# A hybrid encoder block on one core: one raw load queued earlier, another last tile, and another split of its normalisation

## The chip, the cores and the metric

The kernel runs on one core of one Trainium2 chip. A core has five engines with one in-order instruction stream each: TensorE (PE, matrix products; its weight loads are listed as PEld), VectorE (DVE), ScalarE (ACT), GpSimd (POOL) and SyncE (SP), which here issues nearly all DMAs. The metric is the device time of one execution in microseconds (us). Three runs of the kernel before gave 441.77, 443.6 and 445.18 us, a median of 443.6.

## The reference, cut to what matters

One layer on x of 1024 tokens by 1024 columns, in float32:

```
h = x @ W_in                        # sections q_a k_a v_a z_a q_b k_b v_b z_b
y_a = neighborhood_attention(...)   # 8 heads, 8 x 16 window on the 16 x 64 grid, relative bias
y_b = windowed_gqa_with_sink(...)   # 8 query heads, 2 key heads, |i - j| <= 128, rotary
mixed = concat([y_a * silu(z_a), y_b * silu(z_b)])
y = mixed @ W_out
x = layer_norm(2 ** 0.25 * x + y) * gain + bias
```

## The kernel before, in words

Every matrix operand is split into a high and a low float16 half (a "cast" or `hi` on ACT, a subtraction or `lo` on DVE or POOL), and a product of two operands is three PE instructions: high x high, high x low, low x high.

*Prologue.* Six projection groups run, counted in PE products (`run_to`). Small jobs hang on that count through `at(c, fn)`. `w_scale(NPRO)` (L805) is one: it multiplies the sums of the remaining weights' absolute values by a matrix of ones on PE and works out scales on DVE.

*Attention.* A loop over steps i = 0 to 137 (L1576) writes one attention unit of 128 queries per step into the engines' streams: scores on PE (L914, L915), row minimum on DVE (L928), exponential on ACT (L944), the split of the weights on ACT and DVE (L962, L963), a DMA transpose on SP (L965), the products with v (L991), the division (L1000, L1007), a transpose of the head group on PE (L1029) and its product with the gate z (L1035). There are 128 units; the steps after them finish what is in flight. PE's gaps between are filled with the projections and, from step 121 on, with the first products of the output projection.

Beside this, jobs stand in queues per engine. `pop` takes those of a small priority number; `fill_in` takes others when the planner's book says that the engine is free: it adds a cost to `due[engine]` for each job and compares it with `at_step(i)`, the time it gives step i. A job is ready once its dependencies were written out in an earlier step (two steps more behind a DMA) and are booked to be over; an SP entry waits until its dependency's booked end plus 1.0 lies behind. SP takes at most three entries a step from step 118 on, before that step's transpose.

*Output projection.* It is done in 2 x 2 blocks with seven products instead of eight (names q1 to q3, p4, q5 to q7 in `TERMS`, L1286), on sums S1 to S4 of the mixed blocks and T1 to T4 of the weight blocks, each over four parts i = 0 to 3 of the inner dimension. For i = 0 and 1 the T's come ready split (`t_soon`: tiles T of 512 KB). For i = 2 and 3 they come raw: `t_late_load(n)` (L1134) loads 256 KB into one of five buffers, and `t_late(n)` (L1143) queues the cast on ACT and the low half on POOL or DVE. Load n = 0 to 4 follow the weight splits; load 5 (T3, part 3) is queued in `late_loads` (L1560) in step 129 behind two T tiles and one x tile; 5, 6 and 7 each wait for the low half of load 0, 1 and 2, whose buffer they take.

*Closing.* `final` (L1317) is written out by hand. The output has eight row tiles; tile t (0 to 3) and tile 4 + t share their products. A product group is 12 PE instructions into one PSUM bank: `q5(t)`, `q6(t)`, `q7(t)`, `q3(t)`, `p4(t)`, `q2(t)`. `add` (L1333) adds a bank to the row tile in SBUF on DVE, `bn` takes statistics, `begin` aggregates them on DVE and takes the square root on ACT, `norm` normalises: for most tiles DVE does one half of the columns with gain and bias held in PSUM (`gp`, `bp`), and ACT and POOL do the other (`norm_half` multiplies by the gain, adds the bias and sends the half off on SP). For tiles 0, 3 and 4 ACT and POOL do both halves.

The last tile is tile 7. Its first half of columns gets its last product, p4(3), in three pieces of 256, 128 and 128 columns, with statistics by 128 columns. In `norm_last` (L1369) PE keeps itself going with 40 idle products (L1374), then normalises columns 512 to 1024 in PSUM as x * gain - mean * gain + sd * bias, by three pairs of products with diagonal matrices (L1375, L1384, L1385), and ACT scales them out in two pieces (L1391); DVE does columns 0 to 512 (L1386, L1388). `norm_ahead` (L1366) has multiplied the half by the gain on POOL, in between tile 3's instructions there. SP sends 512 and 256 columns, ACT's queue 256.

Of the kernel before, what the change touches and what calls it, by code (L numbers as in the profile page):

```python
# [13 lines left out]
ALU = mybir.AluOpType  # L14
# [56 lines left out]
def hybrid_block(ctx, tc, xT, x, wt, wv, wo, bias, sink, gain, lbias, cos, sin, bmask, out):  # L71
# [403 lines left out]
    with ExitStack() as vctx:  # L475
# [319 lines left out]
        def at(c, fn, *a):  # L795
            events.setdefault(c, []).append(lambda: fn(*a))
# [5 lines left out]
            at(30 + 8 * t, v_part, t)  # L802
        for i in range(NS):
            at(14 + 14 * i + {11: 6, 13: -2, 14: -16}.get(i, 0), sum_w, i)
        at(217, w_scale, NPRO)  # L805
        for c, o in zip((20, 28, 68, 76), T_SUM):
            at(c, t_add, *o)
        at(90, t_store)
# [508 lines left out]
    def final():  # L1317
# [23 lines left out]
        def bn(t, a, c):  # L1341
            o, w = c
            if t not in stats:
                stats[t] = fp.tile([128, 8, 6], F32, name=f"stats{t}", bufs=1)
            b = 128 if t == 7 else 512
            for i in range(w // b):
                n = (512 * a + o) // b + i
                nc.vector.bn_stats(stats[t][:, n, :], xrs[t][:, b * n:b * n + b])

        def row_stats(t):  # L1350
            mv = fp.tile([128, 2], F32, tag="mv", name="mv")
            nc.vector.bn_aggr(mv, stats[t][:, :8 if t == 7 else 2, :])  # L1352
# [8 lines left out]
            nc.vector.tensor_scalar(nmr, mv[:, 0:1], rstd, -1.0, op0=ALU.mult, op1=ALU.mult)  # L1361
            return rstd, nmr

        HP, H1 = slice(512, 1024), slice(0, 512)

        def norm_ahead(t):  # L1366
            nc.gpsimd.tensor_mul(xrs[t][:, HP], xrs[t][:, HP], gb[:, HP])
# [1 line left out]
        def norm_last(t):  # L1369
            ts = slice(128 * t, 128 * t + 128)  # L1370
            xr, pn = xrs[t], bank("t")
            busy = bank("s")
            for _ in range(40):
                nc.tensor.matmul(busy[:, :128], warm, warm, start=True, stop=True)  # L1374
            nc.tensor.matmul(pn, identf, xr[:, HP], start=True, stop=False)  # L1375
            dm, ds = (fp.tile([128, 128], F32, name=n, bufs=1) for n in ("dm", "ds"))
            mv = fp.tile([128, 2], F32, tag="mv", name="mv")
            nc.vector.bn_aggr(mv, stats[t])
            sd = fp.tile([128, 1], F32, tag="sd", name="sd")
            nc.scalar.activation(dm, nident, AF.Copy, scale=mv[:, 0:1])  # L1380
            nc.scalar.activation(sd, mv[:, 1:2], AF.Sqrt, bias=eps)
            nc.scalar.activation(ds, identf, AF.Copy, scale=sd)
            rstd = fp.tile([128, 1], F32, tag="rstd", name="rstd")
            nc.tensor.matmul(pn, dm, gb[:, HP], start=False, stop=False)  # L1384
            nc.tensor.matmul(pn, ds, bb[:, HP], start=False, stop=True)  # L1385
            nc.vector.scalar_tensor_tensor(xr[:, H1], xr[:, H1], mv[:, 0:1], gp, op0=ALU.subtract, op1=ALU.mult)  # L1386
            nc.vector.reciprocal(rstd, sd)
            nc.vector.scalar_tensor_tensor(xr[:, H1], xr[:, H1], rstd, bp, op0=ALU.mult, op1=ALU.add)  # L1388
            nc.sync.dma_start(out[ts, H1], xr[:, H1])
            for h, q in ((slice(512, 768), nc.sync), (slice(768, 1024), nc.scalar)):  # L1390
                nc.scalar.activation(xr[:, h], pn[:, h.start - 512:h.stop - 512], AF.Copy, scale=rstd)  # L1391
                q.dma_start(out[ts, h], xr[:, h])

        begun = []

# [6 lines left out]

        def norm(t, *st_):
            ts = slice(128 * t, 128 * t + 128)
            xr, ha, hb = xrs[t], slice(0, 512), slice(512, 1024)
            mv, sd = st_ or row_stats(t)
            rstd, nmr = row_scale(mv, sd)
            both = t in (0, 3, 4)
            h = slice(0, 1024) if both else hb
            nc.scalar.activation(xr[:, h], xr[:, h], AF.Identity, bias=nmr, scale=rstd)  # L1410
            if not both:
                nc.vector.scalar_tensor_tensor(xr[:, ha], xr[:, ha], mv[:, 0:1], gp, op0=ALU.subtract, op1=ALU.mult)
                nc.vector.scalar_tensor_tensor(xr[:, ha], xr[:, ha], rstd, bp, op0=ALU.mult, op1=ALU.add)
                nc.sync.dma_start(out[ts, ha], xr[:, ha])
            for h in (ha, hb) if both else (hb,):
                if t != 3:
                    norm_half(t, h)

        def norm_half(t, h, between=None):
            xr = xrs[t]  # L1420
            nc.gpsimd.tensor_mul(xr[:, h], xr[:, h], gb[:, h])  # L1421
            if between:
                between()
            nc.gpsimd.tensor_add(xr[:, h], xr[:, h], bb[:, h])
            nc.sync.dma_start(out[128 * t:128 * t + 128, h], xr[:, h])

# [34 lines left out]
        def q3(t):  # L1461
            run("q3", t, cb[t])
            add(t, 1, cb[t], whole=True)
            begin(t)
            if t > 1:
                finish()

        def p4(t):
            run("p4", t, b[t])
            add(4 + t, 0, b[t], whole=True)  # L1470
            begin(4 + t)
            if t > 1:
# [37 lines left out]
        q2(2)  # L1510
        q7(2)
        c11(2)
        q5(3)
        q3(2)
        q6(3)
        p4(2)
        q2(3)
        c11(3)
        q3(3)
        run("q7", 3, b[3])  # L1520
        add(7, 1, b[3])
        add(7, 0, b[3])
        bn(7, 1, (0, 512))
        norm_half(3, slice(0, 512), lambda: norm_ahead(7))
        norm_half(3, slice(512, 1024))
        for c, tag in ((0, 256), "t"), ((256, 128), "s"), ((384, 128), "t"):
            add(7, 0, run("p4", 3, bank(tag), None, c), c, whole=True)
        norm_last(7)

    def m_last(between):  # L1530
        z, za = zt[ZP[3][1]], zt[ZP[3][0]]
# [28 lines left out]
    def late_loads():  # L1560
        t_soon(0)
        x_soon(0)
        t_soon(3)
        t_late_load(5, t_fin[0])
        t_late(5)
        x_soon(4)
        x_soon(1)
        t_late_load(6, t_fin[1])
        t_soon(1)
        t_soon(2)  # L1570
        t_late_load(7, t_fin[2])

    sp_at = []
    clock["step"] = 0
# [1 line left out]
    for i in range(-LD, NU + LO):  # L1576
# [38 lines left out]
        if i == T_AT:  # L1615
            for n in range(5):
                t_late(n)
        if i == 129:
            late_loads()
        if bulk["last"] == i:  # L1620
# [127 lines left out]
```

## Time and profile before

| what | before |
|---|---|
| median of the three runs | 443.6 us |
| the profiled execution | 443.51 us |
| its span, first to last instruction | 441.7 us |
| mean granted clock of PE | 0.994 |
| busy: PE, DVE, ACT, POOL | 430.3, 350.3, 316.3, 295.1 us |
| start of the last output DMA | 437.97 us |

The profile lists, for one execution, when each instruction ran and what ended the idle time before it. In a row of the timeline stand the start, the length, the engine, the line, what it writes from what, and in brackets how long the engine had been idle and who released it. SPq and ACTq are the streams of SP and ACT where they issue DMAs. In the chain of waits stand the start, the length and the work in which the end was waited for.

### The profile page before, as it was taken

Reading aid. Unit: us, or ns where it says so; the run is one execution under the profiler, and the core shown is the slowest. Engines: PE = TensorE matmul, PEld = TensorE weight load, DVE = VectorE, ACT = ScalarE, POOL = GpSimd, SP = SyncE. Lnnn points to the kernel's source line nnn. Section 1 sums busy time; section 2 is a strip of 40 time slices with the busy share of each in tenths; the row PEclk is TensorE's granted clock in tenths of the full one; section 3 lists DMA queues with packets and bytes.
Section 4 is the critical chain, followed back from the end, with each engine's and each line's share of the span. In section 5 each row is a group of like instructions: output and inputs, shape, how many; then the busy total and the mean of one; then the engine's idle time right before and its main releaser. Section 6 shows DMA issues by size and latency. Waiting matters only on the chain.

```text
span 441.7 us, 9455 instructions
## 1 busy us (share of the span) xinstructions
PE 430.3 (97%) x3209; PEld 251.4 (57%) x3209; DVE 350.3 (79%) x870; ACT 316.3 (72%) x681; POOL 295.1 (67%) x303
## 2 busy tenths in 40 slices
PE   9999999999999999999999999999999997999995
PEld 8997754444455656565656565655555653444453
DVE  5988967775978778988898898879879864866684
ACT  4849789678688978888988778888888862743221
POOL 0110085797668656879989898777999796547245
PEclk9999999999999999999999999999999999899999
DMA  7951469995349999987889999898999699803122
GB/s 249 406 195 60 145 226 337 281 332 201 125 123 199 201 169 207 178 182 132 180 160 208 212 193 190 198 209 177 184 191 231 129 179 354 352 24 120 48 96 96
DMA packets 131409, 84.82 MB, mean 192 GB/s; under 512 B 97568, under 2 KB 106656, under 8 KB 131360
## 3 DMA queue, kind: packets, MB, share of 16 engines
q1 hardware_dynamic: 131216, 84.08, 77.0%
q8 instruction: 25, 0.41, 0.4%
q14 instruction: 24, 0.20, 0.1%
q10 hardware_dynamic: 144, 0.13, 0.1%
HBM read 50.60 MB, written 10.52 MB: 138 GB/s over the span
## 4 chain that ended last, share of the span: by engine, by line
PE 76%; DVE 7%; ACT 5%; issue 4%; POOL 4%; DMA 3%; DVEq 0%; POOLq 0%; SPq 0%; ACTq 0%
PE ps_pj L449 38%; PE ps_s L556 6%; PE ps_t L1300 5%; PE ps_t L991 5%; PE ps_pj L1300 5%; PE ps_s L1300 4%; PE ps_pj L556 3%; PE ps_t L556 3%; PE ps_s L915 3%; PE ps_s L914 3%; DVE split L963 2%; DMA tl<-tf 2%; DVE sn L928 1%; POOL tp L1097 1%; ACT ps_s L944 1%
## 5 line engine op out<-in xcount | busy, mean ns | idle before, releaser
L449 PE MATMUL ps_pj<-xf,wh 128*128 128x512 f16 x672 | 201.4, 379 | 0.0
L449 PE MATMUL ps_pj<-xf,wl 128*128 128x512 f16 x336 | 127.3, 379 | 0.0
L449 PEld LDWEIGHTS <-wh 128*128 128x128 f16 x672 | 63.8, 98 | 58.6 <-issue 0.5
L944 ACT ACTIVATE ps_s<-sn,nm 128x321 f32<-128x321 f32 (+3 forms) x128 | 67.7, 529 | 33.9 <-DVE nm L928 32.8
L963 DVE SCALAR_TENSOR_TENSOR split<-ps_s,split 128x320 f16<-128x320 f32 (+2 forms) x128 | 62.7, 490 | 22.1 <-ACT split L962 20.8
L252 POOL TENSOR_SCALAR wr<-wr,wsc 128x512 f32<-128x512 f32 x32 | 24.6, 768 | 57.7 <-ACT wh L247 53.8
L962 ACT ACTIVATE split<-ps_s 128x320 f16<-128x320 f32 (+2 forms) x128 | 55.0, 430 | 1.6
L449 PEld LDWEIGHTS <-wl 128*128 128x128 f16 x336 | 32.9, 98 | 37.8
L253 POOL TENSOR_TENSOR wl<-wr,wh 128x512 f16<-128x512 f32 x32 | 39.9, 1247 | 2.7
L914 PE MATMUL ps_s<-ks,qs 128*128 128x320 f16 (+3 forms) x128 | 38.2, 298 | 0.8 <-DVE split L963 0.8
L915 PE MATMUL ps_s<-ks,qs 128*128 128x320 f16 (+3 forms) x128 | 38.2, 298 | 0.0
L928 DVE CUSTOM_DVE_ANT_0 sn<-ps_s,bias,sg 128x368 f32<-128x368 f32 (+1 forms) x64 | 36.1, 563 | 2.6 <-PE ps_s L915 2.4
L991 PEld LDWEIGHTS <-tr 128*128 128x128 f16 (+1 forms) x1056 | 36.2, 98 | 2.4 <-issue 0.7
L928 DVE CUSTOM_DVE_ANT_0 sn<-ps_s,bm,nsk 128x320 f32<-128x320 f32 (+2 forms) x64 | 36.5, 571 | 0.5
L1300 PEld LDWEIGHTS <-m 128*128 128x128 f16 x192 | 18.1, 98 | 23.6 <-issue 3.9
L1421 POOL TENSOR_TENSOR xr<-xr,gb 128x512 f32<-128x512 f32 x10 | 12.7, 1274 | 24.1 <-ACT xr L1410 24.1
L366 POOL COPY ks<-ks 64x512 f16<-64x512 f16 x40 | 25.7, 643 | 3.9 <-ACT ks L310 1.8
L247 ACT ACTIVATE wh<-wr,wsc 128x512 f16<-128x512 f32 x32 | 22.7, 710 | 1.1 <-DVE wsc L277 1.1
L556 PEld LDWEIGHTS <-xf 128*128 128x128 f16 x192 | 18.6, 98 | 7.3
L915 PEld LDWEIGHTS <-qs 128*128 128x128 f16 x128 | 12.5, 98 | 16.2 <-issue 1.6
L1354 ACT ACTIVATE sd<-mv,eps 128x1 f32<-128x1 f32 x7 | 2.1, 295 | 27.1 <-DVE mv L1352 27.1
L914 PEld LDWEIGHTS <-qs 128*128 128x128 f16 x128 | 12.5, 98 | 15.1
(257 smaller groups left out, 966.3 us busy)
## 6 DMA issues: line engine op xcount, KB each, us to landing
wr<-in_wt SPq DMA_DIRECT2D x32, 256.0 KB, 3.1
ws<-in_wt SPq DMA_DIRECT2D x15, 512.0 KB, 5.6
wor<-in_wo SPq DMA_DIRECT2D x20, 256.0 KB, 3.9
xr<-in_x SPq DMA_DIRECT2D x8, 512.0 KB, 9.0
out<-xr SPq DMA_DIRECT2D x15, 256.0 KB, 2.0
bias<-in_bias SPq DMA_DIRECT2D x8, 440.0 KB, 4.2
wob<-in_wo SPq DMA_DIRECT2D x12, 256.0 KB, 3.9
wvraw<-in_wv SPq DMA_DIRECT2D x9, 320.0 KB, 5.6
```

Of the source, the lines that this page charges most:

```text
L253: nc.gpsimd.tensor_sub(l, raw, h)
L366: nc.gpsimd.tensor_copy(place(t, o, half, col), place(t, a, half, col))
L449: nc.tensor.matmul(ps, a[:, k % 4, :], mv, start=(k == 0 and i == 0), stop=(k == KT - 1 and i == 2))
L556: nc.tensor.matmul(ps[:, :320], lh[:, ts], rh[:, cs], start=(k == ko[0] and i == 0), stop=(k == ko[-1] and i == 2))
L914: nc.tensor.matmul(ps[:, :n], q, sl[0], start=True, stop=False)
L915: nc.tensor.matmul(ps[:, :n], q, sl[1], start=False, stop=True)
L928: nc.vector.tensor_tensor_reduce(sn[:, at0:at0 + n], ps[:, :n], bias_t, sg[:, c:c + 1], init, op0=ALU.add, op1=ALU.min, accum_out=nm)
L944: nc.scalar.activation(pt[:, c], sn[:, c], AF.Exp, bias=nm, scale=-1.0, accum_out=acc)
L962: nc.scalar.activation(h, pt[:, c], AF.Copy, scale=PSCALE)
L963: nc.vector.scalar_tensor_tensor(l, pt[:, c], PSCALE, h, op0=ALU.mult, op1=ALU.subtract)
L991: nc.tensor.matmul(ps[:, w * m:w * m + e], a, b_, start=(i == 0), stop=(i == len(mms) - 1))
L1300: nc.tensor.matmul(ps[:, cs], lh[:, 128 * t:128 * t + 128], rh[:, cs], start=(fresh and e == 0 and n == 0), stop=(e == len(terms) - 1 and ...
```

## The change

*Loads.* Load 5 and its split are queued in step 122, with the splits of loads 0 to 4, instead of in step 129. Loads 6 and 7 are queued one after the other behind one T tile more, ahead of the last T tile.

*Prologue.* `w_scale(NPRO)` hangs on count 224 instead of 217.

*Last tile.* Tile 3 is the last, not 7. Its q5 part is added on its own, q3(3) is the product done in three pieces at the end, and p4(3) and tile 7's statistics come earlier; tile 7 is now one of those that ACT and POOL normalise whole, and `norm_ahead` runs ahead of its four POOL instructions. In every other tile DVE's and ACT's halves change places.

*Split.* In `norm_last` PE normalises columns 0 to 384, and DVE the other 640: 512 as before, and 128 with gain and bias in a PSUM bank `gq`, filled by two ACT copies and also the target of the idle products. ACT scales PE's 384 columns out in one instruction and sends them on its own queue; SP sends 512 and 128.

```
-        at(217, w_scale, NPRO)
+        at(224, w_scale, NPRO)
...
-        HP, H1 = slice(512, 1024), slice(0, 512)
+        HP, HQ, H1 = slice(0, 384), slice(384, 512), slice(512, 1024)
...
-            busy = bank("s")
             for _ in range(40):
-                nc.tensor.matmul(busy[:, :128], warm, warm, start=True, stop=True)
-            nc.tensor.matmul(pn, identf, xr[:, HP], start=True, stop=False)
+                nc.tensor.matmul(gq[:, :128], warm, warm, start=True, stop=True)
+            nc.tensor.matmul(pn[:, HP], identf, xr[:, HP], start=True, stop=False)
...
-            nc.tensor.matmul(pn, dm, gb[:, HP], start=False, stop=False)
-            nc.tensor.matmul(pn, ds, bb[:, HP], start=False, stop=True)
-            nc.vector.scalar_tensor_tensor(xr[:, H1], xr[:, H1], mv[:, 0:1], gp, op0=ALU.subtract, op1=ALU.mult)
-            nc.vector.reciprocal(rstd, sd)
-            nc.vector.scalar_tensor_tensor(xr[:, H1], xr[:, H1], rstd, bp, op0=ALU.mult, op1=ALU.add)
-            nc.sync.dma_start(out[ts, H1], xr[:, H1])
-            for h, q in ((slice(512, 768), nc.sync), (slice(768, 1024), nc.scalar)):
-                nc.scalar.activation(xr[:, h], pn[:, h.start - 512:h.stop - 512], AF.Copy, scale=rstd)
-                q.dma_start(out[ts, h], xr[:, h])
+            nc.tensor.matmul(pn[:, HP], dm, gb[:, HP], start=False, stop=False)
+            nc.tensor.matmul(pn[:, HP], ds, bb[:, HP], start=False, stop=True)
+            halves = (H1, gp, bp), (HQ, gq[:, 128:256], gq[:, 256:384])
+            for h, g, _ in halves:
+                nc.vector.scalar_tensor_tensor(xr[:, h], xr[:, h], mv[:, 0:1], g, op0=ALU.subtract, op1=ALU.mult)
+                if h is H1:
+                    nc.vector.reciprocal(rstd, sd)
+            for h, _, o in halves:
+                nc.vector.scalar_tensor_tensor(xr[:, h], xr[:, h], rstd, o, op0=ALU.mult, op1=ALU.add)
+                if h is H1:
+                    nc.sync.dma_start(out[ts, h], xr[:, h])
+            nc.scalar.activation(xr[:, HP], pn[:, HP], AF.Copy, scale=rstd)
+            nc.sync.dma_start(out[ts, HQ], xr[:, HQ])
+            nc.scalar.dma_start(out[ts, HP], xr[:, HP])
...
-            xr, ha, hb = xrs[t], slice(0, 512), slice(512, 1024)
+            xr, ha, hb = xrs[t], slice(512, 1024), slice(0, 512)
...
-            both = t in (0, 3, 4)
+            both = t in (0, 4, 7)
...
+        gq = bank("s")
+        nc.scalar.copy(gq[:, 128:256], gb[:, HQ])
+        nc.scalar.copy(gq[:, 256:384], bb[:, HQ])
         q5(3)
+        add(3, 1, cb[3])
+        q6(3)
         q3(2)
-        q6(3)
+        q7(3)
         p4(2)
+        p4(3)
         q2(3)
         c11(3)
-        q3(3)
-        run("q7", 3, b[3])
-        add(7, 1, b[3])
-        add(7, 0, b[3])
-        bn(7, 1, (0, 512))
-        norm_half(3, slice(0, 512), lambda: norm_ahead(7))
-        norm_half(3, slice(512, 1024))
+        norm_ahead(3)
+        norm_half(7, slice(0, 512))
+        norm_half(7, slice(512, 1024))
         for c, tag in ((0, 256), "t"), ((256, 128), "s"), ((384, 128), "t"):
-            add(7, 0, run("p4", 3, bank(tag), None, c), c, whole=True)
-        norm_last(7)
+            add(3, 1, run("q3", 3, bank(tag), None, c), c, whole=True)
+        norm_last(3)
...
         t_soon(3)
-        t_late_load(5, t_fin[0])
-        t_late(5)
         x_soon(4)
         x_soon(1)
-        t_late_load(6, t_fin[1])
         t_soon(1)
+        for n in (6, 7):
+            t_late_load(n, t_fin[n - 5])
         t_soon(2)
-        t_late_load(7, t_fin[2])
...
             for n in range(5):
                 t_late(n)
+            t_late_load(5, t_fin[0])
+            t_late(5)
```

More of the change, by code (lines that the diff above doesn't have):

```diff
@@ L1344, in bn @@
                 stats[t] = fp.tile([128, 8, 6], F32, name=f"stats{t}", bufs=1)
-            b = 128 if t == 7 else 512
+            b = 128 if t == 3 else 512
             for i in range(w // b):
@@ L1351, in row_stats @@
             mv = fp.tile([128, 2], F32, tag="mv", name="mv")
-            nc.vector.bn_aggr(mv, stats[t][:, :8 if t == 7 else 2, :])
+            nc.vector.bn_aggr(mv, stats[t][:, :8 if t == 3 else 2, :])
             sd = fp.tile([128, 1], F32, tag="sd", name="sd")
@@ L1415, in norm, with norm_half @@
             for h in (ha, hb) if both else (hb,):
-                if t != 3:
+                if t != 7:
                     norm_half(t, h)
-        def norm_half(t, h, between=None):
+        def norm_half(t, h):
             xr = xrs[t]
             nc.gpsimd.tensor_mul(xr[:, h], xr[:, h], gb[:, h])
-            if between:
-                between()
             nc.gpsimd.tensor_add(xr[:, h], xr[:, h], bb[:, h])
```

## The prediction

> **What bounds the kernel now.** I read the page first, for the slices in which an engine is not full.
>
> ```profile
> PE   9999999999999999999999999999999997999995
> ACT  4849789678688978888988778888888862743221
> PEclk9999999999999999999999999999999999899999
> ```
>
> TensorE (PE) is full in all slices but two: the one from 364 to 375 us (a slice is 441.7 / 40 = 11.04 us) and the last. The granted clock dips in one slice, just behind the first of these, where ScalarE (ACT) falls to 2. So two places can give time: that hole and the tail. The second view is the chain of waits, at the hole.
>
> ```profile
> 363.32 7.59 DMA tl<-tf
> ...
> 373.69 2.75 PE ps_t L1300 x9
> ```
>
> The chain runs through one transfer, raw T load 5, for 7.59 us. Third, the timeline of the same place.
>
> ```profile
> 360.40 1.21 SPq L965 DMA_TRANSPOSE tr<-split  x1
> 361.65 0.58 SPq L1127 DMA_DIRECT2D T<-td  x1
> 361.74 0.62 ACT L1219 CAST s<-z 128x512 f16<-128x512 f32 x1 [1.90 <-DVE z L1242]
> 363.32 0.41 SPq L1139 DMA_DIRECT2D tl<-tf  x1
> 365.46 0.18 DVE L1000 RECIPROCAL ri<-ps_t 128x4 f32<-128x4 f32 x1 [0.28 <-PE ps_t L991]
> 365.68 0.42 DVE L1007 TENSOR_TENSOR on<-ps_t,ri 128x256 f32<-128x256 f32 x1
> 367.85 0.60 PE L1029 MATMUL ps_t<-identf,on 128*128 128x128 f32 x4
> 369.58 0.81 PE L1300 MATMUL ps_t<-tp,s 128*128 128x512 f16 x3
> 370.93 0.72 ACT L1149 ACTIVATE tp<-tl,wsn 128x512 f16<-128x512 f32 x1 [7.56 <-DMA tl<-tf]
> 371.56 0.60 ACT L1219 CAST z<-z 128x512 f16<-128x512 f32 x1
> 372.19 0.79 DVE L1222 TENSOR_TENSOR z<-z 128x512 f16<-128x512 f32 x1 [6.09 <-ACT z L1219]
> 372.90 0.74 DVE L1035 SCALAR_TENSOR_TENSOR z<-ps_t,zc,z 128x512 f32<-128x512 f32 x1
> 373.69 0.59 PE L1300 MATMUL ps_t<-T,m 128*128 128x512 f16 x2 [3.30 <-DVE z L1035]
> ```
>
> Fourth, the busy time by engine of the two stretches behind it (PE, PEld, DVE, ACT, POOL with their counts, then the granted clock, the DMA share and GB/s).
>
> ```profile
> 370.00:375.00 5.00, 1.70 (x9) 0.70 (x8) 2.81 (x5) 2.81 (x4) 3.17 (x3) 1.00 1.03 407
> 375.00:380.00 5.00, 5.00 (x17) 1.94 (x16) 4.96 (x6) 3.96 (x6) 2.72 (x3) 0.66 1.04 421
> ```
>
> ACT stands 7.56 us in front of load 5, which SyncE (SP) issued fourth, behind two T tiles and x tile 0 (the first T tile is the row at 361.65). Behind that wait ACT holds the cast of S4 (371.56), on which VectorE (DVE) holds its low half (372.19), behind which stands the last evacuation of a transposed head group (372.90), which frees the bank that PE wants: PE is idle 3.30 us. Then 17 products run in five microseconds at a mean clock of 0.66, which is 5.00 x 0.34 = 1.70 us lost. The hole costs 3.30 + 1.70 = 5.00 us.
>
> **The change part by part**, against this execution: 443.51 us, 1.81 above its span of 441.7, and 0.1 below the median of 443.6.
>
> **1. Load 5 queued in step 122.** The load hangs on the low half of load 0. I followed the planner's sums in the code: that half is put into the order in step 125 with a booked end of 235.9, an SP entry needs this plus 1.0 to lie behind, and `at_step` gives 236.5 for step 127 and 238.0 for 128. So it goes out in step 128, ahead of that step's single transpose, the row at 360.40. It can't be earlier than step 126, and at the latest it leads step 129, at 361.65. On SP it is moved past three loads and one transpose, and these start about 0.6 us later (its issue of 0.41 and the gaps). The view of the eight raw T loads has this line:
>
> ```profile
> DMA to landing us min/median/max: 3.2/3.9/8.8
> ```
>
> With the median, load 5 lands at 360.4 + 3.9 = 364.3. Its ACT instruction does not go away: by the planner's priorities (1.9 before 2) it is now picked in step 131, ahead of the cast at 361.74, and that cast's low half goes to DVE ahead of the reciprocal at 365.46. So the wait moves onto other work: landing + 0.72 (L1149) + 0.62 (cast) + 0.79 (low half, as at 372.19) + 0.18 + 0.42 and 0.1 of gaps is 367.1; PE asks for it with the transposes at 367.85. A margin of 0.7 us covers the move; past a landing at 365.0 PE waits one for one. The last evacuation then follows the transposes, 368.45 + 0.74 = 369.2, before PE is through at 370.39. So the stall goes whole. What is late next is the cast of A12 behind the scaling of x tile 0.
>
> ```profile
> DMA to landing us min/median/max: 5.4/5.4/5.4
> 372.06 1.05 ACT L1331 ACTIVATE xr<-xr 128x1024 f32<-128x1024 f32 x1
> ```
>
> That is x tile 0 alone, issued at 362.29; 0.6 later it lands at 368.3, is scaled by 369.4 and the cast ends at 370.0. PE wants the A12 low half 9 products of 0.216 (2.59 / 12) and two more after 370.39, at 372.8; DVE needs a subtraction and that low half after 369.2, to about 372.0. Gain 3.30 us; bounds 0 (landing at the row's 8.8) and 3.30.
>
> **2. The clock.** The dip stands directly behind the idle time and nowhere else, so I take its 1.70 us as gone with it; bounds 0 and 1.70. The Trainium skill, "TensorE: Matmul & The Clock Gate", section "What's actually happening", says that the clock halves after an idle window of about 3.4 us whose start is free-running. By that rule an idle time of 3.30 us need not have cost any clock, and the sum would be 1.7 us smaller in an execution whose window falls otherwise; this trace shows the loss behind 3.30 us, and the measurement decides.
>
> **3. Order of the other loads, and the weight scale at 224 instead of 217.** Loads 6 and 7 go behind one T tile more; they feed p4, behind four product groups more: nothing. The scale product:
>
> ```profile
> 106.48 0.19 ACT L790 ACTIVATION_READ_ACCUMULATOR junk<-ws 128x1 f32 x1
> 106.72 0.17 PE L273 MATMUL ps_t<-wm,ones 128*128 128x15 bf16 x1
> ```
>
> It starts 0.05 after the sum it needs (106.67); seven products later it can't wait. That is worth 0.1 at most; against it the scale chain slides behind a rotary step on DVE. Taken as 0, bounds -0.1 and +0.4.
>
> **4. The tail.** The groups of 12 products keep their length and number; tile 7's last two move ahead of tile 3's.
>
> First three rows of the chain, then the timeline, then the row of the DMA issues for the last piece.
>
> ```profile
> 421.51 2.59 PE ps_pj L1300 x12
> 429.28 1.31 PE ps_t L1300 x12
> 435.94 0.87 PE ps_t L1385 x2
> ```
>
> ```profile
> 421.55 0.75 DVE L1336 SCALAR_TENSOR_TENSOR xr<-ps_s,yc,xr 128x512 f32<-128x512 f32 x1 [0.52 <-PE ps_s L1300]
> 422.33 0.69 DVE L1348 BATCH_NORM_STATS2 stats<-xr 128x6 f32<-128x512 f32 x1
> 424.80 0.75 DVE L1413 SCALAR_TENSOR_TENSOR xr<-xr,rstd,ps_s 128x512 f32<-128x512 f32 x1
> 429.43 1.24 ACT L1410 ACTIVATE xr<-xr,nmr,rstd 128x1024 f32<-128x1024 f32 x1 [0.48 <-DVE nmr L1361]
> 431.42 0.47 DVE L1336 SCALAR_TENSOR_TENSOR xr<-ps_t,yc,xr 128x256 f32<-128x256 f32 x1
> 434.01 0.75 DVE L1386 SCALAR_TENSOR_TENSOR xr<-xr,mv,ps_pj 128x512 f32<-128x512 f32 x1
> 435.78 1.26 POOL L1424 TENSOR_TENSOR xr<-xr,bb 128x512 f32<-128x512 f32 x1
> 436.88 0.84 ACT L1391 ACTIVATE xr<-ps_t,rstd 128x256 f32<-128x256 f32 x2 [1.85 <-PE ps_t L1385]
> 437.50 0.38 SPq L1389 DMA_DIRECT2D out<-xr  x1
> 437.97 0.40 SPq L1392 DMA_DIRECT2D out<-xr  x1
> ```
>
> ```profile
> out<-xr SPq DMA_DIRECT2D x1, 128.0 KB, 2.7
> ```
>
> In the times of before: p4(2) ended at 421.5, now at 424.1 (one group of 2.59 later), p4(3) at 426.7, q2(3) at 429.3, the closing pieces from 429.3 as before. DVE takes p4(2)'s result at 424.3 (until then it is at the statistics of q7(3)'s add, queued behind tile 2's scaling) and is through with tile 6 4.0 us later (421.55 to 425.55), at 428.3. Then tile 7: add 0.75, statistics 0.69, and 1.0 to the scale (aggregate, square root on ACT, two small ones), 430.7; then the add for tile 3's half, 431.4. Only then can GpSimd (POOL) multiply tile 3's 384 columns, 1.26 x 384 / 512 = 0.95, and behind this stand tile 7's four instructions at 1.26 and a gap of 0.04: 431.5 + 0.95 + 5.2 = 437.6, where it ended at 437.04. SP is in order: tile 7's last half goes out at 437.6, and behind it, at the pitch of 0.47 between the last two rows, tile 3's 512 columns at 438.1 and the 128 at 438.5, against 437.97. The last piece, 2.7 from issue to landing before, now has half the bytes, which I take as 0.1: +0.4 us.
>
> What the 384 columns save does not reach the end. DVE comes to the closing pieces at 432.1 instead of 431.42, so the mean is 0.7 later, and L1386 would start at 434.7; PE's three pairs of products (0.87 each) shrink by a quarter, 0.65 together, which that uses up, so ACT's one instruction starts near 436.9 again, takes about 0.55 (an estimate, above half of the pair's 0.84) and leaves on its own queue at 437.5, before SP is done. DVE's two instructions more are under the 0.47 of a 256-column one each, so DVE ends by 434.7 + 2 x 0.75 + 2 x 0.47 = 437.1, also before. The two copies of 128 columns into the new bank stand on ACT near 415, in a slice where it is at 2: nothing. Bounds: -0.6 if POOL isn't late and ACT's piece ends the run, +1.2 if POOL starts another 0.7 late.
>
> Sum: 443.51 - 3.30 - 1.70 + 0 + 0.4 = 438.9.
>
> **Rivals.** *The wait moves and lands late (slower).* For it: ACT's wait now stands ahead of two casts, not behind them. At the row's longest, 8.8, load 5 lands at 369.2, the head group is ready at 372.0, PE waits 4.15 us at 367.85 and loses the 1.70 of clock as well: 443.51 - 5.00 + 5.85 + 0.4 = 444.8. It costs from a landing at 365.0 on, and eats the whole gain near 368.8. Against it: only transposes are then ahead of it, where load 5 had three tiles of 512 KB ahead and took 7.6. *The tail is dearer:* POOL and SP as at the upper bound, 438.5 + 1.2 = 439.7, or 440.3 with the prologue's 0.4 and a little more; for it speaks that DVE has 2.6 us of work moved together. *A later load shows:* DMA moves 407 and 421 GB/s from 370 to 380, so the x tiles don't come earlier although PE does; a wait of 1.5 us, or 1.5 and half the clock, gives 440.4 to 441.3. *The clock is lost all the same,* by that free-running window, behind some shorter idle time: 438.9 + 1.7 = 440.6; against it stands the one dip in the whole page. *The load isn't moved in fact:* were it to leave where it does, only the tail remains: 443.9.
>
> **The numbers.** Chances: forecast 0.66 (its own range 438.0 to 439.8), dearer tail 0.12, later load 0.08, clock 0.05, slower than before 0.05, not moved 0.04. The range runs from 437.9 to 442.0: it leaves out the last two, 0.09, and the edges of the first, another 0.1. One per cent of 443.6 is 4.4 us, about what a measurement can tell from no change; the forecast, 4.7 faster, lies just past it. Some two thirds of the forecast's 0.66 fall under 439.2, so faster 0.46, within 1% 0.51; slower would need 448 us, which no single case gives: 0.03.
>
> **What would show it.** Right: load 5's issue ahead of the last transpose, no PE idle time near 370, a clock of 1.00 from 365 to 385, ACT's longest wait for a raw T load under 3 us. The tail is right if SP's last issue waits for POOL and comes 0.5 us later, measured from the end of the closing products. Wrong: PE idle before the transposes (the wait moved), DVE idle on x tile 5 with PE behind it, or an end set by ACT's queue.

## The result, and the profile after

| | before | changed |
|---|---|---|
| median | 444.39 us | 440.91 us |
| lowest and highest | 441.44 to 446.49 us | 439.69 to 442.68 us |
| ratio, with its 95% interval | | 0.9928 (0.9900 to 0.9956) |
| the profiled execution, and its span | 443.51, 441.7 us | 442.68, 440.8 us |

The change is worth some 3.2 us, 0.7%: within one per cent, to which the prediction gave 0.51, against 0.46 for faster. Its number, 438.9, is 2.0 us too low; 440.91 lies in its range.

The profiled execution of the changed kernel is the slowest of those timed, so the two spans say little. The stages have to be read one by one. The slices of the page, of the changed kernel (40 slices of 11.02 us):

```profile
PE   9999999999999999999999999999999999999994
ACT  5849789669659887878897778879688883653122
PEclk9999999999999999999999999999999999999999
```

The 7 in PE's row and the 8 in the clock's row are gone. The timeline of the same place, of the changed kernel:

```profile
363.78 0.53 SPq L1139 DMA_DIRECT2D tl<-tf  x1
364.42 1.20 SPq L965 DMA_TRANSPOSE tr<-split  x1
367.77 0.72 ACT L1149 ACTIVATE tp<-tl,wsn 128x512 f16<-128x512 f32 x1 [5.04 <-DMA tl<-tf]
368.39 0.36 PE L991 MATMUL ps_t<-va,tr 128*128 128x65 f16 x6 [0.28 <-DMA tr<-split]
368.39 0.60 ACT L1219 CAST s<-z 128x512 f16<-128x512 f32 x1
369.03 1.16 DVE L1222 TENSOR_TENSOR s<-z,s 128x512 f16<-128x512 f32 x1 [0.97 <-ACT s L1219]
370.31 0.42 DVE L1007 TENSOR_TENSOR on<-ps_t,ri 128x256 f32<-128x256 f32 x1
371.18 0.60 PE L1029 MATMUL ps_t<-identf,on 128*128 128x128 f32 x4
371.82 0.75 DVE L1035 SCALAR_TENSOR_TENSOR z<-ps_t,zc,z 128x512 f32<-128x512 f32 x1 [1.08 <-PE ps_t L1029]
373.22 0.81 PE L1300 MATMUL ps_t<-tp,s 128*128 128x512 f16 x3
373.87 1.46 PE L1300 MATMUL ps_t<-T,m 128*128 128x512 f16 x6
```

And the stretches behind it (PE, PEld, DVE, ACT, POOL with their counts, clock, DMA share, GB/s):

```profile
370.00:375.00 5.00, 4.87 (x26) 2.33 (x24) 3.88 (x7) 1.60 (x3) 4.66 (x4) 1.00 1.02 406
375.00:380.00 5.00, 5.00 (x24) 2.18 (x23) 4.70 (x6) 4.18 (x6) 2.50 (x2) 1.00 1.01 386
```

Load 5 goes out ahead of the last transpose and lands 4.0 us later, at 367.8. ACT's wait for it now stands in front of the cast (368.39), the low half (369.03) and the division of the head group (L1007), which ends at 370.73; PE asks for that with the last transposes at 371.18. The last evacuation (371.82) follows them, and PE goes from one product group into the next without a wait. PE comes to the last transposes (L1029) at 367.85 before and at 371.18 now. From there to the end of the last closing product it takes 64.08 us before (to 431.93) and 59.39 now (to 430.57): 4.69 us less.

So two things need an explanation: why PE came to that place 3.33 us later, with hardly anything changed ahead of it, and what happened behind the closing products. First the row of PE's last closing product in the timeline of the kernel before, then the tail in that of the changed kernel, and from its DMA issues the row of the last piece:

```profile
431.43 0.50 PE L1300 MATMUL ps_t<-tp,A 128*128 128x128 f16 x6
```

```profile
429.15 0.74 DVE L1336 SCALAR_TENSOR_TENSOR xr<-ps_pj,yc,xr 128x512 f32<-128x512 f32 x1
429.93 0.87 DVE L1348 BATCH_NORM_STATS2 stats<-xr 128x6 f32<-128x128 f32 x4
430.24 0.33 PE L1300 MATMUL ps_t<-z,m 128*128 128x128 f16 x3
430.69 0.99 POOL L1367 TENSOR_TENSOR xr<-xr,gb 128x384 f32<-128x384 f32 x1 [1.82 <-DVE stats L1348]
435.56 1.26 POOL L1426 TENSOR_TENSOR xr<-xr,bb 128x512 f32<-128x512 f32 x1
436.01 0.37 ACTq L1396 DMA_DIRECT2D out<-xr  x1
437.28 0.43 SPq L1393 DMA_DIRECT2D out<-xr  x1
437.80 0.41 SPq L1395 DMA_DIRECT2D out<-xr  x1
```

```profile
out<-xr SPq DMA_DIRECT2D x1, 64.0 KB, 2.0
```

Measured from the end of the last closing product, SP's last issue comes at 7.23 us (437.80 - 430.57), where it came at 6.04 before (437.97 - 431.93); but its landing takes 2.0 instead of 2.7, and the span ends 10.23 us behind the closing products instead of 9.77. The tail is 0.46 dearer.

### The profile page after: what moved, and what is told of

Read it like the earlier page. It is cut to its first block, busy times and chain, and to the rows that moved or that the text cites. A ratio compares the mean times of both kernels' runs of the same rounds, so it can differ in the third digit from the quotient of the medians.

```text
span 440.8 us, 9457 instructions
## 1 busy us (share of the span) xinstructions
PE 429.9 (98%) x3209; PEld 250.9 (57%) x3209; DVE 351.8 (80%) x872; ACT 316.3 (72%) x682; POOL 293.9 (67%) x303
## 4 chain that ended last, share of the span: by engine, by line
PE 58%; DVE 11%; issue 8%; ACT 8%; DMA 7%; POOL 6%; SPq 1%; POOLq 0%; DVEq 0%; ACTq 0%
PE ps_pj L449 21%; PE ps_s L556 6%; PE ps_t L991 5%; PE ps_pj L1300 5%; PE ps_t L1300 4%; PE ps_s L1300 4%; DMA wor<-in_wo 3%; PE ps_pj L556 3%; PE ps_t L556 3%; PE ps_s L914 2%; PE ps_s L915 2%; POOL wl L253 2%; DVE split L963 2%; ACT ps_s L944 1%; DMA T<-td 1%
## 5 line engine op out<-in xcount | busy, mean ns | idle before, releaser
L252 POOL TENSOR_SCALAR wr<-wr,wsc 128x512 f32<-128x512 f32 x32 | 23.7, 741 | 61.6 <-ACT wh L247 59.0
L914 PE MATMUL ps_s<-ks,qs 128*128 128x320 f16 (+3 forms) x128 | 38.1, 298 | 1.7 <-DVE split L963 1.7
L1300 PEld LDWEIGHTS <-m 128*128 128x128 f16 x186 | 17.6, 98 | 19.9 <-POOL m L1222 0.5
L914 PEld LDWEIGHTS <-qs 128*128 128x128 f16 x128 | 12.5, 98 | 15.2 <-DVE qs L318 0.2
L991 PE MATMUL ps_t<-va,tr 128*128 128x65 f16 (+1 forms) x528 | 19.2, 193 | 0.3 <-DMA tr<-split 0.3
```

Of the source, the lines that this page charges most:

```text
L914: nc.tensor.matmul(ps[:, :n], q, sl[0], start=True, stop=False)
L991: nc.tensor.matmul(ps[:, w * m:w * m + e], a, b_, start=(i == 0), stop=(i == len(mms) - 1))
L1300: nc.tensor.matmul(ps[:, cs], lh[:, 128 * t:128 * t + 128], rh[:, cs], start=(fresh and e == 0 and n == 0), stop=(e == len(terms) - 1 and ...
```

## The experiments

Every kernel below was timed beside the kernel before on the same chip, and ratios are against that. e1 to e4, f1 to f4 and g1 to g3 ran on one chip each, three in all, where the kernel before had medians of 443.73, 443.54 and 443.95; medians of different groups are therefore compared through it. The three columns on the right come from each kernel's trace: when PE starts the last transposes (L1029), the time from there to the end of the last closing product, and from there to the end of the span.

| kernel | median, us | ratio (95%) | PE at L1029 | to closing end | to span end |
|---|---|---|---|---|---|
| before | 443.5 to 444.4 | 1 | 367.85 | 64.08 | 9.77 |
| changed | 440.91 | 0.9928 (0.9900 to 0.9956) | 371.18 | 59.39 | 10.23 |
| changed, f1 | 440.97 | 0.9937 (0.9917 to 0.9957) | 368.88 | 59.88 | 10.24 |
| e1, loads alone | 440.57 | 0.9922 (0.9893 to 0.9951) | 367.92 | 59.72 | 9.76 |
| e2, tail alone | 444.57 | 1.0018 (0.9994 to 1.0042) | 370.03 | 65.34 | 10.23 |
| e3, scale at 217 | 440.25 | 0.9914 (0.9885 to 0.9943) | 369.05 | 59.95 | 10.20 |
| e4, hole filled | 443.65 | 0.9991 (0.9972 to 1.0011) | 368.73 | 63.50 | 9.77 |
| g1, scale alone | 443.66 | 0.9992 (0.9972 to 1.0012) | 369.40 | 62.71 | 9.79 |
| g2, scale at 238 | 441.30 | 0.9926 (0.9898 to 0.9954) | 370.59 | 59.71 | 10.20 |
| g3, hole half filled | 443.20 | 0.9974 (0.9953 to 0.9995) | 369.46 | 63.39 | 9.75 |
| f2, SP's order | 440.05 | 0.9917 (0.9892 to 0.9942) | 370.19 | 59.06 | 9.25 |
| f3, last add on DVE | 439.69 | 0.9920 (0.9894 to 0.9946) | 369.44 | 59.50 | 8.96 |
| f4, both and 217 | 440.05 | 0.9915 (0.9894 to 0.9936) | 368.74 | 59.96 | 8.90 |

**e1: the loads alone.** The kernel before with these lines of the change and no others:

```
@@ attention loop
         if i == T_AT:
             for n in range(5):
                 t_late(n)
+            t_late_load(5, t_fin[0])
+            t_late(5)
@@ late_loads
-        t_late_load(5, t_fin[0])
-        t_late(5)
         x_soon(4)
         x_soon(1)
-        t_late_load(6, t_fin[1])
         t_soon(1)
+        for n in (6, 7):
+            t_late_load(n, t_fin[n - 5])
         t_soon(2)
-        t_late_load(7, t_fin[2])
```

> The kernel before with load 5 queued in step 122 and the other closing loads in the new order; tile 7 stays last and the weight scale stays at 217. Theory (the whole gain is the hole and the clock dip behind it, 3.30 + 1.70): 5.0 us under the kernel before, about 439.4 beside 444.4, PE without idle time near 370 and a clock of 1.00 there; the span from the last closing product to the end stays at 9.8 us. Rival 1 (the clock is lost all the same behind something shorter): 3.3 under, 441.1. Rival 2 (load 5 in front costs the attention's transposes, and that is why the changed kernel gained only some 3.4): 3.5 to 4.0 under, PE some 1 us later at the first of the last transposes.

Measured: 440.57, 3.2 under the kernel before beside it. That is rival 1's amount, but not its mechanism, for the clock stays at 1.00 here. In its timeline, PE's rows at the last transposes and at the one wait behind them:

```profile
367.92 0.60 PE L1029 MATMUL ps_t<-identf,on 128*128 128x128 f32 x4
374.32 1.45 PE L1300 MATMUL ps_pj<-T,m 128*128 128x512 f16 x6 [0.35 <-DVE xr L1336]
```

PE reaches the transposes when it did before (367.92, 367.85), where rival 2 wanted it 1 us later. One trace can't decide that, since this place moves by up to 2.3 us between two executions of one kernel (f1 below). A nearer mark can: from the attention's last scores (L914) to these transposes PE takes 11.13 to 11.14 us in all five traces without the edit, 11.35 in e1, and 11.13 to 11.90 in the eight traces with it, 0.3 more in the mean. So the load in front costs the attention something, as rival 2 says, but a third of a microsecond and not one. From the transposes on 4.36 us are gone (64.08 - 59.72), with the clock at 1.00: the hole and the dip went, and a wait of 0.35 came, for VectorE's addition to x tile 0. In the trace, then, nearly what was forecast; in the median 3.2, which suggests that the average execution of the kernel before loses less in the hole than the profiled one did. The next experiments are on that.

**e2: the tail alone.** The changed kernel with loads 5 to 7 back at their old places in `late_loads` and the scale at 217.

> The changed kernel with load 5 back behind two T tiles and x tile 0 and the weight scale at 217: only the new order of the tail and the 384/640 split are left. Theory (the tail is 0.4 to 0.5 dearer: the last issue 1.2 later against the closing products, the last landing 0.7 quicker): 0.5 us over the kernel before, 444.9 beside 444.4, from the last closing product to the end 10.2 us where the kernel before has 9.8; the hole stays at 3.3 with the dip. Rival (the tail is where the missing part of the gain went): 1.0 to 1.6 over, 445.4 to 446.0.

Measured: 1.0018, 0.8 us over, with an interval (-0.3 to +1.9) that holds the theory and the rival alike. The trace decides: 10.23 us from the closing products to the end, the theory's 10.2. Its hole is the dearest of all:

```profile
376.00 2.72 PE L1300 MATMUL ps_t<-T,m 128*128 128x512 f16 x6 [3.43 <-DVE z L1035]
```

PE waited 3.43 us at the place where the kernel before waited 3.30, but the clock was then down for twice as long. Stretches of 3.41 us of e2's trace, cut where its granted clock changes (columns as above):

```profile
371.49:374.91 3.42, 1.08 (x6) 0.39 (x4) 0.41 (x1) 1.67 (x3) 0.77 (x2) 1.00 0.96 349
374.91:378.32 3.41, 2.32 (x6) 0.84 (x6) 3.41 (x6) 1.35 (x3) 2.62 (x2) 0.50 1.05 406
378.32:381.74 3.42, 3.42 (x9) 1.18 (x8) 3.39 (x5) 3.18 (x6) 2.19 (x2) 0.50 1.05 425
381.74:385.15 3.41, 3.41 (x17) 1.54 (x16) 1.16 (x2) 3.41 (x5) 1.18 (x3) 1.00 1.03 413
```

The same cut of the kernel before:

```profile
368.17:371.59 3.42, 2.22 (x12) 0.99 (x11) 0.00 (x0) 0.66 (x2) 0.14 (x1) 1.00 0.98 330
371.59:375.00 3.41, 1.31 (x7) 0.60 (x7) 2.81 (x5) 2.14 (x4) 3.17 (x3) 1.00 1.03 403
375.00:378.41 3.41, 3.41 (x10) 1.17 (x9) 3.38 (x5) 2.37 (x5) 1.39 (x3) 0.50 1.05 423
```

The clock is at exactly a half for one stretch before (1.7 us lost) and for two in e2 (3.4 us lost): the loss comes in whole stretches of 3.41 us. The first such stretch follows one in which PE was busy for 1.31 us (before) or 1.08 us (e2); e2's second follows one with 2.32 us busy at half the clock. The stretches lie on a grid: in both traces 368.64 us, 108 x 3.413, lie between the edge at which the clock first rose (6.36 before, 6.27 in e2; products of 320 columns start 0.27 us apart ahead of it and 0.15 behind) and the one at which it falls (375.00, 374.91). The grid's place against the hole differs: the edge comes 1.31 us behind the hole's end in the kernel before (373.69), and 1.09 ahead of it in e2 (376.00).

**e4 and g3: the hole filled, wholly or in part.** The kernel before, with 48 (e4) or 24 (g3) products of zeros:

```
-        cb = [run("q5", t, bank("t"), range(3)) for t in range(2)]
+        cb = [run("q5", 0, bank("t"), range(3))]
+        for _ in range(48):
+            nc.tensor.matmul(cb[0][:, :128], warm, warm, start=False, stop=False, skip_group_check=True)
+        cb.append(run("q5", 1, bank("t"), range(3)))
```

> The kernel before with 48 products of zeros (128 columns, about 0.06 us each, 2.9 us together) between q5(0) and q5(1), into the bank of q5(0): the wait for the last evacuation stays, but PE is busy in it but for some 0.4 us. They add work that the reference lacks and change no value. Theory (the clock dips because PE stood idle): the stall costs its 3.3 us as before, the granted clock stays at 1.00 from 375 to 380, and the time is 1.7 us under the kernel before, 442.7 beside 444.4 (0.996). Rival (the dip comes from something else at that place, the DMA traffic or the denser products behind): the clock dips as before, and the time stays at 444.4.

> As e4, the kernel before with products of zeros in the hole, but 24 of them (1.4 us), so that PE's idle time is some 1.9 to 2.1 us instead of 3.3 (before) and 0.84 (e4). They add work that the reference lacks and change no value. Theory (the clock is judged over windows of 3.41 us; in the kernel before a window with 2.10 us idle halved it, one with 1.20 did not): with 1.9 to 2.1 us idle the dip is rarer than before or gone; the mean of one minus the clock, 2.2 us of 442 before and 0.8 in e4 (the tail's share), falls to 0.8 to 1.5; time 443.6, as e4. Rival (any idle time of that order brings the dip): 2.0 or more, and 444.0.

PE's row behind the hole, of e4 and then of g3:

```profile
374.80 1.45 PE L1300 MATMUL ps_t<-T,m 128*128 128x512 f16 x6 [0.84 <-DVE z L1035]
378.92 1.46 PE L1300 MATMUL ps_pj<-T,m 128*128 128x512 f16 x6 [0.35 <-DMA xr<-in_x]
```

```profile
375.42 1.46 PE L1300 MATMUL ps_t<-T,m 128*128 128x512 f16 x6 [2.08 <-DVE z L1035]
```

In both traces the clock stays at 1.00, and not in these alone: 40 of 57 timed runs of the kernel before have a mean granted clock under 0.997, and none of the 24 runs of e4 and g3 has. Nothing but products in PE's idle time was added, so the dip comes from that idle time and not from the DMA traffic or the products behind it. In g3's trace the 2.08 us idle were split by the grid into 1.59 and 0.49, the first in this stretch, and did not bring it:

```profile
371.51:374.93 3.42, 1.83 (x27) 1.48 (x25) 1.02 (x2) 2.19 (x3) 1.38 (x2) 1.00 1.03 407
```

The mean over all runs of one minus the clock, times the span, falls from 2.0 us to 0.8 (e4) and 0.7 (g3). But the time did not fall by 1.7. e4 gained 0.4 in the mean of its runs, which can't be told from nothing, and g3 1.2. In e4's trace two waits of 0.20 and 0.35 appear behind the hole, for VectorE's low half of A12 and for x tile 0: with PE at half the clock those two are in time, at full clock they are not. Part of what the dip costs is thus paid in its absence as well. The intervals of e4 and g3 overlap, so that g3 gained more is not shown.

**e3, g1 and g2: the weight scale.** e3 is the changed kernel with 217, g1 the kernel before with 224, g2 the changed kernel with 238. Each is an edit of one line; g1's:

```
-        at(217, w_scale, NPRO)
+        at(224, w_scale, NPRO)
```

> The changed kernel with the weight scale back at 217. Theory (PE reaching the hole 3.6 us later in the changed kernel's trace belongs to that execution, not to the change): as the changed kernel, 440.9 beside 444.4 (0.992), within 0.4. Rival (the scale at 224 holds the rotary steps and the first attention units): 1 to 2 us under it, 439 to 440 (0.988 to 0.990), and PE at the first attention unit 1 us earlier.

> The changed kernel once more, unaltered, for a second trace and beside e3 (the same with the weight scale at 217). Theory (how late PE comes to the hole differs from execution to execution: 367.85 to 371.18 us at the last transposes in the six traces so far): PE there anywhere from 367.5 to 371.5, then 59.4 to 60.0 to the last closing product and 10.2 to the end, no clock dip; 440.3 to 441.3 in the median. Rival (the scale at 224 costs the front part about a microsecond or more): PE at the last transposes past 370.5 again, and a median 0.7 or more over e3's 440.25.

e3 gave 440.25, 3.48 under the kernel before beside it, which is what the changed kernel gave in the result (444.39 - 440.91). Nor does its rival's sign show: with the scale at 217 PE comes to the attention's first scores (L914) at 123.60, with 224 at 123.20. f1, the changed kernel unaltered, comes to L1029 at 368.88, where it came at 371.18: 2.3 us between two executions of one kernel. Both are at the first scores at 123.20, so nothing ahead of them makes the difference, and at the last scores 1.90 apart (357.70, 359.60). Of these, 1.07 are waits of PE for VectorE that the first trace has and f1's has not:

```profile
123.83 0.59 PE L449 MATMUL ps_pj<-xf,wh 128*128 128x512 f16 x2 [0.30 <-DVE z L414]
170.15 0.30 PE L914 MATMUL ps_s<-ks,qs 128*128 128x320 f16 x1 [0.20 <-DVE split L963]
318.84 0.32 PE L914 MATMUL ps_s<-ks,qs 128*128 128x368 f16 x1 [0.40 <-DVE split L963]
319.49 0.63 PE L1029 MATMUL ps_t<-identf,on 128*128 128x128 f32 x4 [0.17 <-DVE on L1007]
```

But f1's median, 440.97, was 0.72 over e3's, just what its rival named, so the scale was tried directly:

> The kernel before with the weight scale at 224 instead of 217 and nothing else. Theory (worth nothing within -0.1 and +0.4): as the kernel before, 1.000, within 0.002. Rival (it explains why the changed kernel, 440.9 and 441.0, lies 0.7 over e3 with 217, 440.25): 0.6 over the kernel before, 1.0014 or more.

> The changed kernel with the weight scale at 238, so three times as far behind the old place (21 products of TensorE, about 4.5 us, instead of 7). Theory (seven products cost nothing): up to 0.5 over the changed kernel, if the attention's first unit begins to wait for the scale at all. Rival (seven products cost 0.6): 1.8 or more over it, 442.7, and PE idle at the first attention unit.

g1 gave 0.9992 (0.9972 to 1.0012). g2, with three times the displacement, gave 441.30, 2.65 under the kernel before beside it where f1 is 2.57 under; the rival needed 1.8 more than f1. Nor is PE idle at g2's first scores. The scale's place is worth nothing that these runs can tell. So the 3.3 us by which the changed kernel's first trace was late at the hole do not belong to the change, but for 0.44 behind the last scores (11.58 us to the transposes, where the kernel before takes 11.14), 0.28 of which are the wait at 368.39. Over all the traces that place is reached between 367.85 and 371.18, with the earliest in the kernel before and the latest in the changed kernel: an unlucky pair. Why VectorE is late in one execution and not in the next was not tried.

g1's trace gave one more thing, a hole without a dip. Its row behind the hole, and its stretches on its own grid:

```profile
374.68 1.46 PE L1300 MATMUL ps_t<-T,m 128*128 128x512 f16 x6 [2.74 <-DVE z L1035]
```

```profile
369.48:372.90 3.42, 2.46 (x14) 1.23 (x13) 0.00 (x0) 0.98 (x2) 0.42 (x2) 1.00 0.98 308
372.90:376.31 3.41, 1.63 (x8) 0.78 (x8) 3.13 (x5) 1.82 (x3) 3.22 (x3) 1.00 1.03 407
376.31:379.72 3.41, 2.86 (x14) 1.05 (x12) 3.38 (x6) 2.69 (x5) 1.49 (x2) 1.00 1.05 419
```

2.74 us idle lay across an edge of the grid, 0.96 on the one side and 1.78 on the other, and the clock stayed up.

**f2, f3, f4: the tail.** f2 is the changed kernel with these lines; the third argument makes `norm_half` multiply and add without its DMA:

```
         norm_ahead(3)
         norm_half(7, slice(0, 512))
-        norm_half(7, slice(512, 1024))
+        norm_half(7, slice(512, 1024), False)
...
         norm_last(3)
+        nc.sync.dma_start(out[896:1024, 512:], xrs[7][:, 512:])
```

In f3 the third argument leaves out POOL's addition too, and the last addition of that half is `nc.vector.tensor_add(xrs[7][:, 512:], xrs[7][:, 512:], bp)` behind `norm_last(3)`. f4 adds to f3 the scale at 217, and POOL's first multiplication on tile 7 ahead of `norm_ahead(3)`.

> The changed kernel with the output of tile 7's second half issued last, behind the two pieces of tile 3. Theory (SP's last issue waits behind POOL, and the last landing counts): tile 3's pieces leave near closing end + 4.6 and 5.1, tile 7's half when POOL is through, at closing end + 6.3 instead of the 7.2 of the last issue now; but the last transfer is 256 KB instead of 64, so 0.7 of these 0.95 us go again: from the last closing product to the end 9.9 to 10.0 instead of 10.2, in the time 0.2 to 0.3 less than the changed kernel. Rival (the end is set by the transfers, not by when they are issued): 10.2 as now.

> As f2, and the last addition on tile 7 (bias of its second half) on VectorE behind its own last instruction instead of on POOL (1.26 us there). Theory: POOL is through at closing end + 4.9, VectorE adds in some 0.75 and SP issues near + 5.7; from the last closing product to the end 9.3 to 9.4, 0.8 to 0.9 under the changed kernel. Rival (ACT's piece or the landing of tile 3's pieces ends the run by then): 9.8 to 10.0.

> As f3, with the weight scale at 217 and POOL's first multiplication on tile 7 ahead of the one on tile 3 that waits for the statistics. Theory: POOL starts 0.1 to 0.2 earlier, 9.1 to 9.3 from the last closing product to the end, some 1.0 under the changed kernel: 439.9 beside 443.7 to 444.4 before (0.990). Rival on the scale (217 is worth a microsecond or more by itself): 438.9 or less. Rival on POOL's order (the multiplication on tile 3 then comes too late for TensorE): 9.5 or more.

SP's last rows, of f2:

```profile
434.15 0.41 SPq L1395 DMA_DIRECT2D out<-xr  x1
434.24 1.26 POOL L1426 TENSOR_TENSOR xr<-xr,bb 128x512 f32<-128x512 f32 x1
435.53 0.33 SPq L1534 DMA_DIRECT2D out<-xr  x1
```

and of f3:

```profile
433.89 0.69 DVE L1534 TENSOR_TENSOR xr<-xr,ps_s 128x512 f32<-128x512 f32 x1 [0.23 <-POOL xr L1425]
434.38 0.37 ACTq L1396 DMA_DIRECT2D out<-xr  x1
434.61 0.33 SPq L1535 DMA_DIRECT2D out<-xr  x1
```

The issues came where they were expected: 6.28 us behind the closing products in f2 (435.53 - 429.25) and 5.67 in f3 (434.61 - 428.94), after 7.23 in the changed kernel. So POOL's chain, and SP behind it, set the end. What I had wrong is the landing. f2's last piece of 256 KB took 2.0 us, as the changed kernel's 64 KB did, and not 2.7, so its tail is 9.25 and not 9.9; f3 and f4 are 0.3 to 0.4 and 0.2 to 0.4 shorter than expected, with last landings of 2.4. f4's POOL begins 0.1 earlier by its order, and PE's wait for the later multiplication (0.24 us) costs nothing; its tail of 8.90 is the shortest, 1.33 under the changed kernel's and 0.87 under that of the kernel before. In the medians f2 to f4 are 0.9 to 1.3 under the changed kernel timed beside them (440.97); the intervals of the ratios overlap, so that they are faster is shown by the traces and not by the times alone.

## Why the prediction was right or wrong

**1. The load: right in its mechanism, with two small terms missing.** The load left ahead of the last transpose, as worked out from the planner, took 4.0 us to land where the median of 3.9 was used, and the stall at L1300 is gone in every kernel with the edit. The margin at the transposes was put at 0.7; it is 0.45 in the first trace (371.18 - 370.73) and 0.74 in f1's (368.88 - 368.14). ACT's wait for the load did not go under 3 us, as the list of signs wanted: it is 5.04, and harmless, since the division that stands behind it is ready before PE asks for it. What was late next was named rightly, A12 and x tile 0, but priced at nothing: in e3 and f1 PE waits for both. f1's rows:

```profile
374.06 1.04 PE L1300 MATMUL ps_s<-wo,A 128*128 128x512 f16 x4 [0.26 <-DVE A L1544]
375.45 1.46 PE L1300 MATMUL ps_pj<-T,m 128*128 128x512 f16 x6 [0.35 <-DVE xr L1336]
```

And one consumer was not followed: the load pushes the last transpose back on SP, and in three of the eight traces with the edit PE then waits for it, 0.28 us in the changed kernel's row at 368.39, 0.60 and 0.53 in f2 and f3; in the five without the edit it never does. These waits lie ahead of L1029, so the table's column from there hides them. With one wait of 0.38 for a T tile in f3, all these waits make 0.3 to 0.9 us per execution, 0.5 in the mean of the eight traces; this is the rival "a later load shows", at a third of its price and in addition to the forecast instead of in its place. In the rival of the late landing, the 368.8 near which it was to eat the whole gain does not follow from its terms: a gain of 4.6 is gone with a wait of 2.9 us and the clock lost, so from a landing at 367.9. Nothing else rests on it.

**2. The clock: right for the trace, mis-sized for the mean.** The term "I take its 1.70 us as gone" came from one execution and went into a forecast of a median. The traces show 0 (g1), 1.7 (before) and 3.4 (e2) for nearly the same hole, by where it falls on the grid. Over 57 timed runs of the kernel before, one minus the mean granted clock, times the span, comes to 2.0 us; over the 76 runs of the kernels without a hole or with a filled one it comes to 0.8, which is the end of the span, where PE has stopped. The difference, 1.2 us, is the clock that the dip takes on average. It shows in the time: 15 runs with a clock of 1.00 took 443.1 us in the mean, 8 runs with 0.990 took 445.5. How much of the 1.2 us comes back when the dip goes is less sure, since e4 got back 0.4 and g3 1.2. The rule quoted from the Trainium skill ("TensorE: Matmul & The Clock Gate", "What's actually happening") has a free-running window of about 3.4 us; the length of the stretches (3.41 us) and their grid agree with that. It also has the clock fall after an idle window, and in this the measurement differs: 2.10 us idle out of 3.41 halved the next stretch (before, 371.59 to 375.00), and 1.78 did not (g1, 372.90 to 376.31). So a stall of 3.30 us can cost clock without filling a window, but need not. The prediction says that the loss depends on how the window falls, and still gave that doubt a chance only as a clock lost in the changed kernel, where it belonged to the kernel before.

**3. The scale and the order of the other loads: right**, nothing that can be told.

**4. The tail: the right sum by luck, from two errors that cancel.** Forecast +0.4, measured +0.46. The first error is in the step "then the add for tile 3's half, 431.4. Only then can GpSimd multiply". Behind the add stand the statistics of that half, four instructions and 0.87 us on DVE, and POOL overwrites what they read, so it waits for them: the row at 430.69, released by L1348. Counted from the closing products, POOL starts at +0.12 where the forecast has 431.5 - 431.93 = -0.43, and the last issue comes at +7.23 where it has 438.5 - 431.93 = +6.57. The second error is "which I take as 0.1": the smaller last piece lands 0.7 sooner. The issue alone reached the upper bound of 1.2 (7.23 - 6.04 = 1.19), and no bound allowed for a landing 0.7 sooner. PE, ACT and DVE were done before SP, as forecast.

**The sum.** The kernel before takes 444.0 in the mean of the 57 runs, 0.5 more than its profiled execution, from which the forecast counted. Taking from this the mean of the three stalls seen (3.30, 3.43 and 2.74: 3.16) and the mean dip (1.2), and adding 0.5 for the waits and 0.46 for the tail, gives 440.6; the changed kernel's mean over 16 runs is 440.97. The 2.0 us by which the forecast was low are thus mostly the execution (0.5), the dip (0.5) and the waits (0.5), with 0.06 from the tail and 0.14 from the stall. The last 0.4 stays open; the waits are put high rather than low in this, since g1, the kernel before without a dip, has 0.55 of them too.

## What to carry to other kernels

A stall read off one trace is a fact of that execution: before it is turned into a forecast, set the trace's own time and its mean clock against the other runs, because a dip that comes in whole stretches of 3.41 us is there in one execution and not in the next, and work hidden behind it shows when it goes. Compare two traces from landmarks within them (here the last scores, the last transposes and the last closing product) and not by their spans, and set a landmark ahead of everything that the change touches. In a tail, ask what reads a tile that an engine is about to overwrite, not only what writes it, and in which order an in-order queue sends its last pieces: changing that order alone took 1 us off the tail here.

## What was not expected of the hardware

- The clock of PE halved for a whole stretch of 3.41 us where the stretch before had 2.10 us of idle time in it (before) or 2.34 (e2), and not at 1.78 (g1) or 1.59 (g3), one trace each; once it was down, a stretch with 2.32 us busy at half the clock (e2, 374.91 to 378.32) did not bring it up again, and one with 3.41 did. At full clock a stretch with 2.22 busy kept it up (before, 368.17 to 371.59).
- The last output DMA took 2.0 us from issue to landing for 64 KB (changed kernel) and for 256 KB (f2) alike. It took 2.4 in f3, with 192 KB on ACT's queue 0.23 us earlier, and 2.7 in the kernel before, with 256 and 128 KB in the 0.47 us ahead of it. That transfers issued beside it stretch a landing fits these but is not shown: the 64 KB had 256 KB 0.52 us ahead on their own queue. The Trainium skill, "DMA: Bandwidth & Descriptors", section "Anatomy of one DMA — SWDGE (gpsimd) path", has a fixed cost of about 2.0 us for transfers from GpSimd, most of it completion and not setup, and adds the bytes at 436 GB/s. The 2.0 agrees, though these transfers leave from SP's queue; the 0.45 us more that its formula, as an estimate, gives 256 KB over 64 do not show, and no run here splits the 2.0 us.
- With nothing altered, PE comes to the same instruction, some 370 us into the program, 2.3 us apart in two executions (f1 and the changed kernel). It is at the attention's first scores at the same time in both, and 1.07 us are short waits for VectorE that only one of them has; what brings these stays open.
